# Operand parts side by side for each k-tile, and 18 more projection slabs in a two-matmul form

## The chip, the cores and the metric

The kernel runs on one core of a Trainium2 chip, in one launch. The metric is the device time of that launch in microseconds (us), as a median over runs. A core has five engines with a queue each: PE (TensorE, matmuls, with its weight loads shown apart as PEld), DVE (VectorE), ACT (ScalarE), POOL (GpSimd) and SP (which here issues transfers). Each engine works through its own queue in order and waits on semaphores for the others. SBUF is the on-chip memory with 128 partitions; PSUM holds what PE writes, in eight banks of 512 float32 a partition.

## What is computed

Two transformer blocks on 256 tokens of width 1024, all in float32. Rotary embedding, norms and the scan of the first layer are left out here.

```python
def reference(x, ...):
    x = first_block(x, ...)          # even layer (window attention + scan), FFN, odd layer, FFN
    return second_block(x, mem, ...)

def second_block(x, mem, ...):
    x = x + 0.5 * swiglu(rmsnorm(x, ffn1_norm), ffn1_w_gate, ffn1_w_up, ffn1_w_down)
    z = rmsnorm(x, mix_norm) @ w_in
    z_sgu = gelu(z[..., :2 * D_SGU])                 # gates u and values v
    ...                                              # q, k, v of the dilated attention
    y_a = chunked_spatial_gating(z_sgu, ...)
    y_b = dilated_mixture_attention(q, k, v)
    x = x + concatenate([rmsnorm(y_a), rmsnorm(y_b)]) @ w_out
    x = x + memory_cross_attention(rmsnorm(x), rmsnorm(mem), wq, wk, wv, wo)
    x = x + 0.5 * swiglu(rmsnorm(x, ffn2_norm), ffn2_w_gate, ffn2_w_up, ffn2_w_down)
    return rmsnorm(x, final_norm)

def memory_cross_attention(h, m, wq, wk, wv, wo):
    q, k, v = h @ wq, m @ wk, m @ wv                 # 4 heads of 256
    p = softmax(q @ k.T / 16)
    return (p @ v) @ wo
```

The odd layer of the first block is a stick-breaking attention: `A[t,s] = beta_ts * prod(1 - beta_tj)` over `s < j < t`, with the product done as a sum of softplus values that a matmul with a triangular matrix adds up. Four FFNs (gate, up, down; 2816 wide) hold most of the arithmetic.

## The kernel before

**Two parts for each number.** PE takes its operands in a rounded 32-bit type, so each float32 operand is held as a high and a low part, and a product is hi·hi + hi·lo + lo·hi. Weights come in slabs of 128 x 2048 (`slab`, transfer at L277); ACT casts each half of a slab to its high part `whi` (L293) and DVE subtracts to get `wlo` (L295), two slabs ahead of their use, in 5 buffers each. Both engines do this for every slab beside their other work. Activations are transposed: features on partitions, the 256 tokens along the free axis. An operand tile `a` is `[128, 2 parts, 4 k-tiles, 256]` (`operand`), two of them for the 1024 features; the hidden tiles `h0` to `h10` of an FFN are `[128, 2 parts, 2 k-tiles, 256]`.

**Two ways of a product.** `mm3` (L320 to L322) is three matmuls of 256 moving columns with a weight load each: whi·hi, whi·lo, wlo·hi. `mm2` (L366, L367) is two: wlo·hi with 256 columns, then whi against hi and lo at once with 512 columns, into a whole PSUM bank, whose second half then holds whi·lo and has to be added to the first. With the parts outermost in the tile, the 512 columns of L367 are two runs of 256. Only the FFNs use `mm2`; all other projections go through `gemm_feat` or `gemm_tok` with `mm3`. In `gemm_feat` one slab of 256 features fills one bank (the two blocks b of 128 features in its halves), half of the k-tiles first for both blocks, then the other half. One DVE multiplication by the norm's factors (`scaled`, L482; L1350 for the gates of the mix) takes it out of PSUM. In the FFN each block of 128 features has a bank of its own; `half` takes it out with an ACT copy of the second half (L525, into a tile `half` with 4 buffers) and a DVE addition (L526). In `gemm_tok` tokens are the stationary side and 512 weights lie contiguous as moving columns.

**Stages.** Even layer, FFN, odd layer, FFN, FFN, mix (spatial gating and dilated attention, with the memory's norm and the first of its projections between), cross attention, FFN, final norm. Strings give the order in which pieces are written: `ODD = "q0 k0 k1 q1 a00 k2 k3 l00 a01 l01 q2 q3 a10 ..."` (q, k, v: projections by slab; a: scores and softplus, L1191 to L1211; l: the triangular sums, L1218), `MIX = "x N v w y r0 r1 u0 10 u1 00 K0 11 g0 01 12 g1 13 K1 K2 K3"` (u: gates; two digits: steps of the dilated attention, L587 to L625; g: gating, L1357; N, K: the memory's norm and the cross attention's keys), `CROSS = "q0 q1 s00 s10 t00 t10 q2 v00 v10 q3 s11 s01 w0 ..."` (q: projections; s: scores L1408 and softmax L1413 to L1420; t: transposes of the probabilities, helper L401, with the copy out of PSUM at L1429; v: products with the values, L1440; w: output projection). A scheduler then sets every engine's final order from its own estimates, so the order in the program can differ from the strings.

**Banks.** `ps(tag)` hands out banks in turn: 2 with the tag `mm`, 4 `acc`, 2 `tr`. Projections, scores of the dilated attention and its q·k share `mm`; a new user waits until the user two before has been read out.

Of the kernel before, what the change touches and what calls it, by code (L numbers as in the profile page):

```python
# [8 lines left out]
F32 = mybir.dt.float32  # L9
F32R = mybir.dt.float32r  # L10
# [3 lines left out]
ALU = mybir.AluOpType  # L14
AX = mybir.AxisListType

P = 128
# [211 lines left out]
class Parts(tuple):  # L229


    def __new__(cls, x):
        self = super().__new__(cls, (x[:, 0], x[:, 1]))
        self.both = x
        return self


class Kernel:
# [85 lines left out]
    def operand(self, pool=None, tag="a"):  # L324

        if pool is not None:
            x = self.t(pool, [P, 2, 4, 256], tag, F32R)
        else:
            x = self.t(self.ap4, [P, 2, 4, 256], "a", F32R, bufs=self.A_BUFS)
        return Parts(x)  # L330

    def lhs(self, ops, k, t):
# [29 lines left out]
    def mm2(self, out, w, x, first, last):  # L362


        mm = self.nc.tensor.matmul
        mm(out[:, 0, :], w[1], x[:, 0], start=first, stop=False, skip_group_check=True)  # L366
        mm(out, w[0], x, start=False, stop=last, skip_group_check=True)  # L367

    def gemm_out(self, acc, w, ops, ks, first, last, done=None):

# [106 lines left out]
        rb, rs = self.inv_rms(sqs, D, 1e-6, tag)  # L477
        return ops, rb, rs

    def scaled(self, dst, rb):  # L480

        return lambda c, ps: self.nc.vector.tensor_tensor(  # L482
            dst[:, 2 * c:2 * c + 2, :], ps, rb.unsqueeze(1).to_broadcast([P, 2, 256]), ALU.mult)


    def memory(self, f, how, pool=None):
        nc = self.nc
        c = int(f[1:] or 0)
        if f[0] == "N":
            mem = self.t(self.wp, [P, 2048], "raw", bufs=2).rearrange("p (b t) -> p b t", b=8)  # L490
            self.load_feat(mem, self.a["mem"], nc.sync)
            self.mops, self.mrb, self.mrs = self.norm(mem, 8, "mrb", haste=False, pool=pool, soon=how[1])
        elif f[0] == "K":
            if not self.kt:
                self.kt = self.t(self.late, [P, 8, 256], "kt")
            self.gemm_feat(self.mops, "cross_wk", 0, c * 256, 256,
                           self.scaled(self.kt[:, 2 * c:2 * c + 2, :], self.mrb), how[0])
# [13 lines left out]


    def ffn(self, kind, layer, gain, factor):
        nc = self.nc
# [3 lines left out]
        rb2 = rb.unsqueeze(1).to_broadcast([P, 2, 256])  # L518
        hs = []

        def half(ps, dst):

            v = ps.rearrange("p (i t) -> p i t", i=2)
            y = self.t(fp, [P, 256], "half", bufs=4)
            nc.scalar.copy(y, v[:, 1])  # L525
            nc.vector.tensor_tensor(dst, v[:, 0], y, ALU.add)  # L526

        def products(name, c, tag, evac):
            w = self.slab(f"{kind}_{name}", layer, "f", 0, c * 256)
            for b in range(2):  # L530
                ps = self.ps(tag)
                out = ps.rearrange("p (i t) -> p i t", i=2)
                for k in range(8):
                    self.mm2(out, w(k * 256 + b * P, P), ops[k // 4].both[:, :, k % 4, :], k == 0, k == 7)
                evac(b, ps)

        for c in range(11):
            sg = self.t(fp, [P, 2, 256], "sg", bufs=2)
            h = self.t(fp, [P, 2, 256], "h", bufs=2)
            x = self.t(fp, [P, 2, 2, 256], f"h{c}", F32R)  # L540
            hs.append(x)

            products("gate", c, "acc", lambda b, ps, sg=sg: half(ps, sg[:, b]))
# [3 lines left out]
            products("up", c, "mm", lambda b, ps, h=h: half(ps, h[:, b]))  # L547
            nc.vector.tensor_tensor(h, h, sg, ALU.mult)
            nc.scalar.copy(x[:, 0], h)
            nc.vector.tensor_tensor(x[:, 1], h, x[:, 0].bitcast(F32), ALU.subtract)  # L550


        n = 0
        for o in range(8):
            ps = self.ps("acc")
            out = ps.rearrange("p (i t) -> p i t", i=2)
            for k in range(22):
                if n % 16 == 0:
                    w = self.slab(f"{kind}_down", layer, "d", n, 0, ahead=LASTF if n == 160 else None)
                self.mm2(out, w(n % 16 * P, P), hs[k // 2][:, :, k % 2, :], k == 0, k == 21)  # L560
                n += 1
            with self.tc.high_priority(offset=self.HASTE):
                y = self.t(fp, [P, 256], "y", bufs=2)
                x = self.xt[:, o, :]
                nc.vector.scalar_tensor_tensor(y, out[:, 0], factor, x, ALU.mult, ALU.add)
                nc.vector.scalar_tensor_tensor(x, out[:, 1], factor, y, ALU.mult, ALU.add)
        stack.close()


# [533 lines left out]
    def ssm_gate(self, ep, gy):  # L1103
        nc = self.nc
        flat = lambda x: x.rearrange("p a n -> p (a n)")
        yt = self.t(ep, [P, 8, 4, 32], "s1")
        hi, lo = self.operand()
        for h in range(2):
            ps = self.ps("tr")
            for t in range(4):  # L1110
# [46 lines left out]
    def odd(self):  # L1157
# [84 lines left out]
        for f in ODD.split():  # L1242
# [2 lines left out]
                toks(ops, "odd_w_in", 2048, c, v, rs)  # L1245
            elif f[0] in "kq":
                dst, base, r = (kt, 1024, rb) if f[0] == "k" else (qt, 0, rb8)
                self.gemm_feat(ops, "odd_w_in", 0, base + c * 256, 256,
                               self.scaled(dst[:, 2 * c:2 * c + 2, :], r), "acc" if f in OACC else "mm")
            elif f[0] == "a":  # L1250
                scores(*divmod(c, 10))
            elif f[0] == "l":
# [11 lines left out]
    def mix(self):  # L1264
# [80 lines left out]

        su = self.t(mp, [P, 4, 256], "su")

        def gates(c, ps):
            d = su[:, 2 * c:2 * c + 2, :]
            nc.vector.tensor_tensor(d, ps, rb.unsqueeze(1).to_broadcast([P, 2, 256]), ALU.mult)  # L1350
            nc.scalar.activation(d, d, AF.Gelu)

        def gating(t):
# [17 lines left out]
        for f in MIX.split():  # L1371
# [8 lines left out]
            elif f[0] == "r":  # L1380
                att[c] = dilated(c)
            elif f[0] == "u":
                self.gemm_feat(ops, "w_in", 0, c * 256, 256, lambda _, ps: gates(c, ps))
            elif f[0] == "g":
                gating(c)
            elif f[0] in "NKW":
# [7 lines left out]
    def cross(self):  # L1394
# [51 lines left out]
        for n, f in enumerate(CROSS.split()):  # L1446
            c = int(f[1])
            if f[0] == "q":
                self.gemm_feat(ops, "cross_wq", 0, c * 256, 256,
                               self.scaled(qt[:, 2 * c:2 * c + 2, :], rb), "mm" if c < CQ else "acc")  # L1450
            elif f[0] == "s":
                scores(c, int(f[2]))
            elif f[0] == "t":
# [105 lines left out]
```

## Time and profile before

| | |
|---|---|
| runs | 1245.78, 1247.03, 1249.15 us (median 1247.03) |
| profiled execution | 1243.83 us, its span on the core 1242.1 us |
| PE | busy 1211.7 us, 98% of the span, 7686 matmul records |
| DVE, ACT, POOL | 868.8 us (70%), 676.6 us (54%), 211.2 us (17%) |
| granted TensorE clock | 0.986 of full speed over the span; lower only in the first tenth |
| weights moved | 205.57 MB read from HBM, 167 GB/s |

The page divides the span in 40 slices of 31 us. From the fourth on PE shows the highest digit in every slice but the last, while DVE is at 5 to 8 tenths and ACT at 4 to 6. Matmuls are pipelined: the time that a row gives for one (0.28 us for 256 columns) is longer than the distance between the starts of two in a row, and that distance is what a stream costs. So matmuls are read below by start times. The chain that ended last lies on PE for 92% of the span.

### The profile page before, as it was taken

Reading aid. Unit: us, or ns where it says so; the run is one execution under the profiler, and the core shown is the slowest. Engines: PE = TensorE matmul, PEld = TensorE weight load, DVE = VectorE, ACT = ScalarE, POOL = GpSimd, SP = SyncE. Lnnn points to the kernel's source line nnn. Section 1 sums busy time; section 2 is a strip of 40 time slices with the busy share of each in tenths; the row PEclk is TensorE's granted clock in tenths of the full one; section 3 lists DMA queues with packets and bytes.
Section 4 is the critical chain, followed back from the end, with each engine's and each line's share of the span. In section 5 each row is a group of like instructions: output and inputs, shape, how many; then the busy total and the mean of one; then the engine's idle time right before and its main releaser. Section 6 shows DMA issues by size and latency. Waiting matters only on the chain.

```text
span 1242.1 us, 19044 instructions
## 1 busy us (share of the span) xinstructions
PE 1211.7 (98%) x7686; PEld 1072.7 (86%) x7686; DVE 868.8 (70%) x1191; ACT 676.6 (54%) x1052; POOL 211.2 (17%) x177
## 2 busy tenths in 40 slices
PE   6889999999999999999999999999999999999997
PEld 6777998888899879888888888888889999888886
DVE  8978588777665647877766867766866656777752
ACT  6543566565446755655545655545664545655542
POOL 7665021110010002101001110002201101111000
PEclk9978999999999999999999999999999999999998
DMA  6541355555553325455654545646633434555551
GB/s 208 172 158 53 139 172 194 180 201 203 180 197 110 131 68 204 170 187 186 216 191 174 196 177 198 204 174 212 209 131 103 155 118 139 190 183 201 204 200 38
DMA packets 36776, 208.86 MB, mean 168 GB/s; under 512 B 3920, under 2 KB 9808, under 8 KB 12752
## 3 DMA queue, kind: packets, MB, share of 16 engines
q1 hardware_dynamic: 35824, 205.48, 47.7%
q0 software_dynamic: 576, 1.64, 0.5%
q8 instruction: 60, 0.98, 0.3%
q10 hardware_dynamic: 288, 0.52, 0.1%
q14 instruction: 28, 0.23, 0.1%
HBM read 205.57 MB, written 2.06 MB: 167 GB/s over the span
## 4 chain that ended last, share of the span: by engine, by line
PE 92%; DVE 5%; DMA 1%; issue 1%; ACT 1%; POOL 0%; DVEq 0%; ACTq 0%
PE acc L367 26%; PE acc L366 13%; PE mm L367 13%; PE mm L366 7%; PE mm L320 4%; PE mm L322 4%; PE mm L321 4%; PE acc L322 4%; PE acc L321 4%; PE acc L320 4%; PE mm L591 1%; PE tr L401 1%; PE acc L1191 1%; DVE wlo L295 1%; PE acc L625 1%; DVE a L454 1%
## 5 line engine op out<-in xcount | busy, mean ns | idle before, releaser
L295 DVE TENSOR_TENSOR wlo<-raw,whi 128x1024 fp32r<-128x1024 f32 (+1 forms) x378 | 472.0, 1251 | 225.1 <-ACT whi L293 223.6
L293 ACT CAST whi<-raw 128x1024 fp32r<-128x1024 f32 (+1 forms) x378 | 392.4, 1043 | 280.8 <-DMA raw<-in_wts 111.2
L367 PE MATMUL acc<-h,whi 128*128 128x512 f32 x704 | 247.8, 397 | 0.0
L367 PE MATMUL mm<-a,whi 128*128 128x512 f32 x704 | 247.0, 392 | 0.0
L367 PE MATMUL acc<-a,whi 128*128 128x512 f32 x704 | 246.0, 392 | 0.0
L366 PE MATMUL acc<-h,wlo 128*128 128x256 f32 x704 | 196.9, 281 | 0.0
L366 PE MATMUL mm<-a,wlo 128*128 128x256 f32 x704 | 196.6, 281 | 0.0
L366 PE MATMUL acc<-a,wlo 128*128 128x256 f32 x704 | 196.3, 280 | 0.0
L367 PEld LDWEIGHTS acc<-h,whi 128*128 128x128 f32 x704 | 131.9, 188 | 32.0
L367 PEld LDWEIGHTS mm<-a,whi 128*128 128x128 f32 x704 | 131.5, 187 | 28.5
L367 PEld LDWEIGHTS acc<-a,whi 128*128 128x128 f32 x704 | 130.9, 187 | 28.2
L366 PEld LDWEIGHTS acc<-a,wlo 128*128 128x128 f32 x704 | 133.0, 189 | 1.0
L366 PEld LDWEIGHTS acc<-h,wlo 128*128 128x128 f32 x704 | 132.9, 189 | 0.3
L366 PEld LDWEIGHTS mm<-a,wlo 128*128 128x128 f32 x704 | 132.6, 189 | 0.2
L546 POOL TENSOR_TENSOR sg<-sg,rb 128x512 f32<-128x512 f32 x44 | 58.2, 1326 | 388.8 <-ACT sg L545 379.2
L463 POOL TENSOR_TENSOR ssq<-ssq,sq 128x512 f32<-128x512 f32 x26 | 39.7, 1528 | 416.7 <-ACT sq L461 253.2
L320 PE MATMUL mm<-a,whi 128*128 128x256 f32 x224 | 66.4, 298 | 6.7 <-ACT whi L293 6.7
L321 PE MATMUL acc<-a,whi 128*128 128x256 f32 x240 | 67.4, 284 | 0.0
L322 PE MATMUL acc<-a,wlo 128*128 128x256 f32 x240 | 67.1, 285 | 0.0
L322 PE MATMUL mm<-a,wlo 128*128 128x256 f32 x224 | 66.1, 296 | 0.8 <-DVE wlo L295 0.7
L320 PE MATMUL acc<-a,whi 128*128 128x256 f32 x240 | 66.0, 286 | 0.0
L321 PE MATMUL mm<-a,whi 128*128 128x256 f32 x224 | 65.8, 295 | 0.0
(371 smaller groups left out, 1951.5 us busy)
## 6 DMA issues: line engine op xcount, KB each, us to landing
raw<-in_wts SPq DMA_DIRECT2D x187, 1024.0 KB, 4.9
raw<-in_mem SPq DMA_DIRECT2D x4, 512.0 KB, 5.6
eb<-lag SPq DMA_DIRECT2D x4, 512.0 KB, 4.8
x<-in_x SPq DMA_DIRECT2D x4, 256.0 KB, 5.3
raw<-in_wts SPq DMA_DIRECT2D x4, 256.0 KB, 5.6
sprm<-in_prm SPq DMA_DIRECT2D x1, 512.0 KB, 9.1
ud<-s SPq DMA_DIRECT2D x1, 512.0 KB, 2.6
uu<-ud SPq DMA_DIRECT2D x8, 64.0 KB, 5.3
```

Source lines behind the costliest of these rows:

```text
L293: nc.scalar.copy(hi[:, c:c + n], src)
L295: nc.vector.tensor_tensor(lo[:, c:c + n], src, hi[:, c:c + n].bitcast(F32), ALU.subtract)
L320: mm(out, a[0], b[0], start=start, stop=False, skip_group_check=True)
L321: mm(out, a[0], b[1], start=False, stop=False, skip_group_check=True)
L322: mm(out, a[1], b[0], start=False, stop=stop, skip_group_check=True)
L366: mm(out[:, 0, :], w[1], x[:, 0], start=first, stop=False, skip_group_check=True)
L367: mm(out, w[0], x, start=False, stop=last, skip_group_check=True)
L401: self.nc.tensor.transpose(out, in_, self.ident[:k, :k])
L454: lo = nc.vector.scalar_tensor_tensor(lo, x[:, b, :], g, hi.bitcast(F32), ALU.mult, ALU.subtract).ins
L463: nc.gpsimd.tensor_tensor(ssq, ssq, q, ALU.add)
L546: nc.gpsimd.tensor_tensor(sg, sg, rb2, ALU.mult)
L591: nc.tensor.matmul(scv[:, i, :], qt[r, qb, t * P:(t + 1) * P], kt[r, kblock(qb), 0:keys], start=False, stop=(i == per - 1))
```

## The change

The operand tiles are laid out with the two parts of a k-tile side by side: `[128, 4 k-tiles, 2 parts, 256]`, and the hidden tiles of the FFN `[128, 2 k-tiles, 2 parts, 256]`. The 512 columns of the second matmul of `mm2` are then one run (`both(k)`). The projections `cross_wk` (4 slabs), `odd_w_in` for q and k (8), the two slabs of the mix's gates in `w_in`, and `cross_wq` (4) go from `gemm_feat` with `mm3` to `gemm_scaled`, which uses `mm2` as the FFN does: 18 slabs, 16 products of k-tile and block each. A slab then takes two banks, one for each block, one after the other. It is taken out with `halves` for each block, whose temporary now comes from the tag `sq` (2 buffers of 512, shared with the squares of the norms), and one multiplication in SBUF for both blocks. The FFNs call the same helpers. One tile of the even layer (`ssm_gate`) keeps the old layout.

```diff
 class Parts(tuple):
-        self = super().__new__(cls, (x[:, 0], x[:, 1]))
-        self.both = x
+        self = super().__new__(cls, (x[:, :, 0], x[:, :, 1]))
+        self.tile = x
         return self
+    def both(self, k):
+        return self.tile[:, k].rearrange("p i t -> p (i t)")
...
-            x = self.t(self.ap4, [P, 2, 4, 256], "a", F32R, bufs=self.A_BUFS)
+            x = self.t(self.ap4, [P, 4, 2, 256], "a", F32R, bufs=self.A_BUFS)
...
-        mm(out[:, 0, :], w[1], x[:, 0], start=first, stop=False, skip_group_check=True)
+        mm(out[:, :256], w[1], x[:, :256], start=first, stop=False, skip_group_check=True)
         mm(out, w[0], x, start=False, stop=last, skip_group_check=True)
+    def halves(self, ps, dst):
+        y = self.t(self.wk, [P, 512], "sq", bufs=2)[:, :256]
+        self.nc.scalar.copy(y, ps[:, 256:])
+        self.nc.vector.tensor_tensor(dst, ps[:, :256], y, ALU.add)
+    def gemm_wide(self, ops, name, layer, n0, dst, tag="mm"):
+        w = self.slab(name, layer, "f", 0, n0)
+        for b in range(2):
+            ps = self.ps(tag)
+            for k in range(8):
+                self.mm2(ps, w(k * 256 + b * P, P), ops[k // 4].both(k % 4), k == 0, k == 7)
+            self.halves(ps, dst[:, b])
...
-    def scaled(self, dst, rb):
-        return lambda c, ps: self.nc.vector.tensor_tensor(
-            dst[:, 2 * c:2 * c + 2, :], ps, rb.unsqueeze(1).to_broadcast([P, 2, 256]), ALU.mult)
+    def gemm_scaled(self, ops, name, layer, n0, dst, rb, tag="mm"):
+        self.gemm_wide(ops, name, layer, n0, dst, tag)
+        self.nc.vector.tensor_tensor(dst, dst, rb.unsqueeze(1).to_broadcast([P, 2, 256]), ALU.mult)
...
-            x = self.t(fp, [P, 2, 2, 256], f"h{c}", F32R)
+            x = Parts(self.t(fp, [P, 2, 2, 256], f"h{c}", F32R))
...
-        def gates(c, ps):
+        def gates(c):
             d = su[:, 2 * c:2 * c + 2, :]
-            nc.vector.tensor_tensor(d, ps, rb.unsqueeze(1).to_broadcast([P, 2, 256]), ALU.mult)
+            self.gemm_scaled(ops, "w_in", 0, c * 256, d, rb)
             nc.scalar.activation(d, d, AF.Gelu)
...
-                self.gemm_feat(ops, "cross_wq", 0, c * 256, 256,
-                               self.scaled(qt[:, 2 * c:2 * c + 2, :], rb), "mm" if c < CQ else "acc")
+                self.gemm_scaled(ops, "cross_wq", 0, c * 256, qt[:, 2 * c:2 * c + 2, :], rb,
+                                 "mm" if c < CQ else "acc")
```

With fewer matmuls to place, the scheduler sets other orders. In the FFNs PE's order is the same as before. PE's queue has 6897 rows before and 6608 after.

PE of the kernel before, in the cross attention, around the first scores (`mm` <- `kt`, `qt`, tiles 1661 and 1665; `acc_1686` is q's fourth slab; L401 transposes the probabilities that come of the scores):

```order
L322 MATMUL acc_1678_9756<-a_1637_9539,wlo_1653_9591 128x256
L1408 MATMUL mm_1661_9704<-kt_1543_8849,qt_1646_9581 128x256 x2
L1408 MATMUL mm_1665_9718<-kt_1543_8849,qt_1646_9581 128x256 x4
L320 MATMUL acc_1686_9838<-a_1636_9538,whi_1656_9646 128x256
L321 MATMUL acc_1686_9838<-a_1636_9538,whi_1656_9646 128x256
...
L322 MATMUL acc_1686_9838<-a_1637_9539,wlo_1659_9651 128x256
L401 MATMUL tr_1669_9732<-ident_6_80,prob_1664_9713 128x128 x4
```

The same place on PE after (L1409 are the scores, L419 the transposes, `acc_1739` the second block of q's fourth slab):

```order
L369 MATMUL acc_1739_9705<-a_1679_9413,wlo_1704_9516 128x256
L370 MATMUL acc_1739_9705<-a_1679_9413,whi_1703_9515 128x512
L1409 MATMUL mm_1713_9574<-kt_1573_8759,qt_1688_9455 128x256 x2
L1409 MATMUL mm_1709_9560<-kt_1573_8759,qt_1688_9455 128x256 x2
L419 MATMUL tr_1717_9588<-ident_6_80,prob_1712_9569 128x128 x4
L419 MATMUL tr_1721_9595<-ident_6_80,prob_1716_9583 128x128 x4
L1441 MATMUL mm_1730_9653<-probt_1718_9593,mv0_111_578 128x128
```

Before, 39 matmuls of q's fourth slab stand between the last scores and the first transposes; after, that slab stands ahead of the scores and nothing stands between.

DVE after, from the last addition of q's fourth slab to the first probabilities (L1414 to L1421 are the softmax, L298 is the low part of a weight slab, L501 q's multiplication):

```order
L376 TENSOR_TENSOR qt_1688_9455<-acc_1739_9705,sq_1740_9722 128x256
L1414 TENSOR_REDUCE mx2_1710_9565<-mm_1709_9560 128x2
L298 TENSOR_TENSOR wlo_1755_9761<-raw_1753_9758,whi_1754_9760 128x1024
L501 TENSOR_TENSOR qt_1688_9455<-qt_1688_9455,rb_1687_9453 128x512
L1415 TENSOR_SCALAR mx2_1710_9565<-mx2_1710_9565 128x2
L1414 TENSOR_REDUCE mx2_1714_9579<-mm_1713_9574 128x2
L1415 TENSOR_SCALAR mx2_1714_9579<-mx2_1714_9579 128x2
L1420 RECIPROCAL den2_1711_9566<-den2_1711_9566 128x2
L1421 TENSOR_TENSOR prob_1712_9569<-prob_1712_9569,den2_1711_9566 128x512
```

Before, DVE had no split and no multiplication between the first reduction and the first probabilities; after, one of each stands there.

PE after, in the mix, at the gates' second slab (`mm_1556` is the bank of the dilated attention's first scores; `mm_1565` and `mm_1567` are the two blocks of the slab, with `mm` handing out two banks in turn):

```order
L591 MATMUL mm_1556_8657<-kt_1456_8189,qt_1455_8188 128x256 x2
L369 MATMUL mm_1565_8690<-a_1440_8138,wlo_1524_8520 128x256
L370 MATMUL mm_1565_8690<-a_1440_8138,whi_1523_8519 128x512
...
L369 MATMUL mm_1567_8710<-a_1440_8138,wlo_1524_8520 128x256
L370 MATMUL mm_1567_8710<-a_1440_8138,whi_1523_8519 128x512
...
L419 MATMUL tr_1558_8669<-ident_6_80,prob_1557_8664 128x128 x4
L587 MATMUL mm_1569_8732<-dilh_1434_8124,identr_7_82 128x512
```

Before, the slab's 48 matmuls went into one bank and stood between the scores and the next user of the scores' bank (L587); after, the slab's second block is that next user, with 16 matmuls between.

## Rows read from the trace of the kernel before

**Rows 1.** The page: PE's share of the span, and the granted clock in 40 slices.

```profile
PE 1211.7 (98%) x7686; PEld 1072.7 (86%) x7686; DVE 868.8 (70%) x1191; ACT 676.6 (54%) x1052; POOL 211.2 (17%) x177
...
PEclk9978999999999999999999999999999999999998
```

**Rows 2.** Timeline of PE: start, us, engine, line, tiles, columns; two-matmul pairs with operand `a`.

```profile
230.11 0.28 PE L366 MATMUL mm<-a,wlo 128*128 128x256 f32 x1
230.23 0.39 PE L367 MATMUL mm<-a,whi 128*128 128x512 f32 x1
...
236.01 0.28 PE L366 MATMUL acc<-a,wlo 128*128 128x256 f32 x1
```

**Rows 3.** Timeline of PE in the down projection of the first FFN.

```profile
289.05 0.28 PE L366 MATMUL acc<-h,wlo 128*128 128x256 f32 x1
...
296.67 0.40 PE L366 MATMUL acc<-h,wlo 128*128 128x256 f32 x2
...
345.04 0.28 PE L366 MATMUL acc<-h,wlo 128*128 128x256 f32 x1
...
350.34 0.28 PE L366 MATMUL acc<-h,wlo 128*128 128x256 f32 x1
```

**Rows 4.** Timeline of PE, three-matmul products in the odd layer's first projection.

```profile
351.05 0.28 PE L320 MATMUL mm<-a,whi 128*128 128x256 f32 x1
...
351.77 0.28 PE L320 MATMUL mm<-a,whi 128*128 128x256 f32 x1
```

**Rows 5.** Timeline of PE, matmuls with 512 contiguous moving columns.

```profile
419.27 0.39 PE L321 MATMUL mm<-wlo,a 128*128 128x512 f32 x1
...
424.94 0.39 PE L322 MATMUL mm<-whi,a 128*128 128x512 f32 x1
```

**Rows 6.** Groups from 350 us to 1045 us: busy, mean ns | idle before; bank read-outs.

```profile
L526 DVE TENSOR_TENSOR h<-mm,half 128x256 f32<-128x256 f32 x44 | 18.1, 414 | 0.0
...
L525 ACT COPY half<-mm 128x256 f32<-128x256 f32 x44 | 16.1, 365 | 7.9 <-PE mm L367 7.7
...
L482 DVE TENSOR_TENSOR qt<-mm,rb 128x512 f32<-128x512 f32 x6 | 4.0, 683 | 0.7 <-PE mm L322 0.7
```

**Rows 7.** Waits of PE from 350.6 to 1045.4 us: total, times, longest.

```profile
PE acc L625 <- ACT prob L619: 1.1, 2, 0.7
```

**Rows 8.** Timeline of the cross attention's first scores and softmax.

```profile
1002.69 1.46 PE L1408 MATMUL mm<-kt,qt 128*128 128x256 f32 x6
...
1003.97 0.68 DVE L1413 TENSOR_REDUCE mx<-mm 128x2 f32<-128x512 f32 x1
...
1006.19 0.69 DVE L1420 TENSOR_TENSOR prob<-prob,den 128x512 f32<-128x512 f32 x1
...
1007.10 0.69 DVE L1420 TENSOR_TENSOR prob<-prob,den 128x512 f32<-128x512 f32 x1
...
1008.65 0.60 PE L401 MATMUL tr<-ident,prob 128*128 128x128 f32 x4
```

**Rows 9.** Timeline of the mix at the dilated attention's first scores.

```profile
903.78 1.13 PE L591 MATMUL mm<-kt,qt 64*128 64x256 f32 x4
...
905.32 1.23 DVE L295 TENSOR_TENSOR wlo<-raw,whi 128x1024 fp32r<-128x1024 f32 x1 [0.82 <-ACT whi L293]
...
909.55 0.20 ACT L605 ACTIVATION_READ_ACCUMULATOR prob<-mm,mneg 128x1 f32 x1
...
910.68 0.40 PE L587 MATMUL mm<-dilh,identr 128*128 128x512 f32 x1
```

**Rows 10.** Timeline of the mix: the sum of a norm's squares.

```profile
928.13 0.73 POOL L1310 TENSOR_TENSOR sq<-sq 128x256 f32<-128x256 f32 x1 [40.08 <-ACT sq L1309]
```

**Rows 11.** Timeline of the odd layer's first scores, softplus and triangular sums.

```profile
378.69 1.60 PE L1191 MATMUL acc<-qt,kt 64*128 64x128 f32 x12
...
385.83 1.13 ACT L1210 CAST sph<-sp 128x512 fp32r<-128x512 f32 x2
...
390.40 0.40 PE L1218 MATMUL acc<-sph,trih 128*128 128x512 f32 x1
```

More of the change, by code (lines that the diff above doesn't have):

```diff
@@ L326, in operand @@
         if pool is not None:
-            x = self.t(pool, [P, 2, 4, 256], tag, F32R)
+            x = self.t(pool, [P, 4, 2, 256], tag, F32R)
         else:
-            x = self.t(self.ap4, [P, 2, 4, 256], "a", F32R, bufs=self.A_BUFS)
+            x = self.t(self.ap4, [P, 4, 2, 256], "a", F32R, bufs=self.A_BUFS)
         return Parts(x)
@@ L495, in memory @@
                 self.kt = self.t(self.late, [P, 8, 256], "kt")
-            self.gemm_feat(self.mops, "cross_wk", 0, c * 256, 256,
-                           self.scaled(self.kt[:, 2 * c:2 * c + 2, :], self.mrb), how[0])
+            self.gemm_scaled(self.mops, "cross_wk", 0, c * 256, self.kt[:, 2 * c:2 * c + 2, :], self.mrb, how[0])
         else:
@@ L519, in ffn @@
         hs = []
[L521 to L535, printed above, removed]
         for c in range(11):
@@ L539, in ffn @@
             h = self.t(fp, [P, 2, 256], "h", bufs=2)
-            x = self.t(fp, [P, 2, 2, 256], f"h{c}", F32R)
+            x = Parts(self.t(fp, [P, 2, 2, 256], f"h{c}", F32R))
             hs.append(x)
-            products("gate", c, "acc", lambda b, ps, sg=sg: half(ps, sg[:, b]))
+            self.gemm_wide(ops, f"{kind}_gate", layer, c * 256, sg, "acc")
             nc.vector.tensor_tensor(sg, sg, rb2, ALU.mult)
@@ L546, in ffn @@
             nc.gpsimd.tensor_tensor(sg, sg, rb2, ALU.mult)
-            products("up", c, "mm", lambda b, ps, h=h: half(ps, h[:, b]))
+            self.gemm_wide(ops, f"{kind}_up", layer, c * 256, h)
             nc.vector.tensor_tensor(h, h, sg, ALU.mult)
-            nc.scalar.copy(x[:, 0], h)
-            nc.vector.tensor_tensor(x[:, 1], h, x[:, 0].bitcast(F32), ALU.subtract)
+            nc.scalar.copy(x[0], h)
+            nc.vector.tensor_tensor(x[1], h, x[0].bitcast(F32), ALU.subtract)
         n = 0
@@ L555, in ffn @@
             ps = self.ps("acc")
-            out = ps.rearrange("p (i t) -> p i t", i=2)
             for k in range(22):
@@ L559, in ffn @@
                     w = self.slab(f"{kind}_down", layer, "d", n, 0, ahead=LASTF if n == 160 else None)
-                self.mm2(out, w(n % 16 * P, P), hs[k // 2][:, :, k % 2, :], k == 0, k == 21)
+                self.mm2(ps, w(n % 16 * P, P), hs[k // 2].both(k % 2), k == 0, k == 21)
                 n += 1
@@ L564, in ffn @@
                 x = self.xt[:, o, :]
-                nc.vector.scalar_tensor_tensor(y, out[:, 0], factor, x, ALU.mult, ALU.add)
-                nc.vector.scalar_tensor_tensor(x, out[:, 1], factor, y, ALU.mult, ALU.add)
+                nc.vector.scalar_tensor_tensor(y, ps[:, :256], factor, x, ALU.mult, ALU.add)
+                nc.vector.scalar_tensor_tensor(x, ps[:, 256:], factor, y, ALU.mult, ALU.add)
         stack.close()
@@ L1106, in ssm_gate @@
         yt = self.t(ep, [P, 8, 4, 32], "s1")
-        hi, lo = self.operand()
+        x = self.t(self.ap4, [P, 2, 4, 256], "a", F32R, bufs=self.A_BUFS)
+        hi, lo = x[:, 0], x[:, 1]
         for h in range(2):
@@ L1247, in odd @@
                 dst, base, r = (kt, 1024, rb) if f[0] == "k" else (qt, 0, rb8)
-                self.gemm_feat(ops, "odd_w_in", 0, base + c * 256, 256,
-                               self.scaled(dst[:, 2 * c:2 * c + 2, :], r), "acc" if f in OACC else "mm")
+                self.gemm_scaled(ops, "odd_w_in", 0, base + c * 256, dst[:, 2 * c:2 * c + 2, :], r,
+                                 "acc" if f in OACC else "mm")
             elif f[0] == "a":
@@ L1382, in mix @@
             elif f[0] == "u":
-                self.gemm_feat(ops, "w_in", 0, c * 256, 256, lambda _, ps: gates(c, ps))
+                gates(c)
             elif f[0] == "g":
```

## The prediction

> **What bounds the kernel now.** I read the page first: PE is busy 98% of the span, at full granted clock in all slices but the first few [rows 1]. So a price is paid on PE, either as the distance between the starts of two matmuls or as a gap in its queue. The next view is therefore PE's timeline, read by start times. A pair of `mm2` on operand `a` runs in 5.90 us / 17 = 347 ns over 17 pairs [rows 2]. In the down projection 22 pairs run in 7.62 us, 346 ns each; at 296.67 two matmuls of 256 follow each other, since there PE's order breaks the alternation, and from then to the end of the stage the pairs run slower, 15 of them in 5.30 us, 353 ns each [rows 3]. So the two-run operand is not slow as such; it falls into a slower rhythm after a broken alternation and stays there. A triple of `mm3` takes 0.72 us / 2 = 360 ns, so 120 ns for 256 columns [rows 4], and a contiguous 512 takes 5.67 us / 25 = 227 ns [rows 5]. At last I read PE's waits between the second FFN's neighbours: in the odd layer, the mix and the cross attention they come to little over a microsecond [rows 7]. These stages are covered almost without a gap, and how much cover each wait has is the question for this change.
>
> **The matmuls removed.** 18 slabs of 16 products go from 360 to 347 ns: 288 x 13 ns = **-3.7 us**. No column is saved; 512 + 256 stream as before, and what goes is the start of one matmul (two of 120 against one of 227). The Trainium skill ("TensorE: Matmul & The Clock Gate", section "Back-to-back issue gap") gives a lone matmul N/2.4 + 2.5 ns, by which the removal would be worth 288 x 2.5 ns, an estimate of 0.7 us; rows 4 and 5 show a larger fixed part, 13 ns over N/2.4, and I go by them.
>
> **The layout.** Contiguous parts give 120 + 227 = 347 ns, what the two-run pair already takes in its fast rhythm. What they may end is the slow one. Its price is 353 - 347 = 6 ns on 704 - 4 x 22 = 616 pairs of the four down projections (8 x 22 x 4), taking the other three like the one shown: **3.7 us**. For its end speaks that streams with one shape of contiguous rows hold 227 ns [rows 5]; against it, that I see no contiguous 512 alternate with 256. I give the end a little better than even. FFN orders don't change, so nothing else moves there.
>
> **Read-outs.** A slab's one DVE multiplication (0.68 us) becomes two ACT copies (0.37), two DVE additions (0.41) and the multiplication [rows 6]: 0.73 us of ACT and 0.83 of DVE in each 5.6 us slab. Both engines have room on the average [rows 1], so the sum of it costs nothing. Where a chain through them releases PE it counts, and so do the shorter distances in PE's new order. Those are the next three terms.
>
> **Cross attention.** Before, the first reduction starts at 1003.97 and the first probabilities end at 1006.88, 2.91 us later; the second end at 1007.79; the transposes stand at 1008.65, behind q's fourth slab [rows 8]. After, that slab is ahead of the scores, and PE has nothing between. DVE has in the same chain a split (1.23 us) [rows 9] and q's multiplication (0.69) [rows 6]: 2.91 + 1.23 + 0.69 = 4.8 us from the reduction, which can start about when PE issues its last score. PE stands about 4.8 us; the second transposes come 0.9 us after the first, whose own 0.36 us fill a part, so 0.5 more. **+5.4 us**. Bounds: 3 (split and multiplication turn out to lie elsewhere) and 6.
>
> **Mix.** Before, the first scores' bank is released by the last exponential at 909.75, and PE comes back to it at 910.68, after 48 matmuls in the 5.8 us since the scores [rows 9]. After, the second block of the gates' slab needs that bank when 16 matmuls, 2.8 us, have passed: 904.9 + 2.8 = 907.7, against 909.75. That is 2.0 us, and 2.4 with the other block's copy and addition ahead in the queues. The same for the first key slab behind the next exponentials, with a shorter chain, 0.7. Later in the stage transposes, the product with the values and the norm's sums stand in direct sequence; each pair waits for an ACT copy as L625 does already, 0.7 at worst [rows 7], two of them 1.4; a third waits for a square on ACT and an addition on POOL, some 0.7 each [rows 7, 10], 1.4. The place of the 1.1 us before falls away, of which I take back 0.7. **+5.2 us**, bounds 2 and 8 (from one such wait to all with the splits in the chain).
>
> **Odd layer.** Scores end at 380.3 and the first `sph` at 386.4: 6.1 us, covered four times over since the sums come at 390.40 [rows 11]. After, 15 pairs (5.2 us) and a few scores are left between, so 0.7 us, and up to 1.8 with the new addition and copy ahead. **+1.2 us**, bounds 0 and 3.5.
>
> **The sum.** New waits 5.4 + 5.2 + 1.2 = 11.8; with -3.7 that is **+8.1 us** where the slow rhythm stays and **+4.4 us** where it ends. On the profiled execution's 1243.83 that gives 1248.2; against the median of the runs, which lies 3.2 us above that execution, 1247.03 + 4.4 = **1251.4 us**.
>
> **Rivals.**
> - *The slow rhythm stays.* Then 1247.03 + 8.1 = 1255.1. For it: the break in the FFN's order is still there. Against: rows 5.
> - *Contiguous columns are faster than the fast rhythm; the kernel gets faster.* In a two-run pair the 256 takes 0.12 and the 512 the rest, 347 - 117 = 230 ns [rows 2]; if the 230 holds 3 ns for the second run and contiguous rows give 117 + 227 = 343, all 2112 pairs of the FFNs and the 288 new ones gain 3.8 ns, 9.1 us: 1251.4 - 9.1 = 1242.3. From 3.4 ns a pair on it is faster by more than 0.3% (4.4 + 3.7 = 8.1 us over 2400 pairs). For it: 230 against 227. Against: 256 in a stream takes 120, not 117 [rows 4], so the 3 ns seem only to change sides. The Trainium skill ("Advanced Engine Details and Errata", section "PSUM Cachelines") says that non-contiguous access patterns slow matmuls markedly, which would put the result here; the fast two-run pairs of rows 2 don't bear it out for this operand, the slow ones of rows 3 may.
> - *The cover is there after all.* The waits are half of what I sum, 5.9, because ACT and DVE run further ahead: 1247.03 + 8.1 - 5.9 - 3.7 = 1245.5 with the slow rhythm gone; no change. For it: both engines are at two thirds. Against: in the cross attention PE's order leaves nothing to run.
> - *All pairs fall into the slow rhythm*, if a contiguous 512 meets a 256 badly: 6 ns on 1408 + 288 more pairs and no gain, 1255.1 + 10.2 = 1265.3.
>
> That the change doesn't do what it says is no rival: PE's queue loses 289 rows.
>
> **How the numbers follow.** Likeliest is the forecast, new waits with the slow rhythm gone, 40%; the rhythm stays, 30%; contiguous faster, 12%; cover, 14%; all slow, 4%. A measurement of this kernel can tell about 0.3%, 3.7 us, from no change. The forecast lies just beyond that, and its waits are uncertain by some 4 us: 0.24 slower, 0.15 same, 0.01 faster. The second gives 0.27 and 0.03; the third 0.09 faster, 0.03 same; the fourth 0.10 same, 0.04 faster; the last 0.04 slower. Together 0.14 faster, 0.31 same, 0.55 slower. The range goes from 1243.0 (the third at its weaker end) to 1258.0 (the second with its waits 3 us longer).
>
> **What would show it.** The pairs in the down projection after the broken alternation: 347 or 353 ns. The waits of PE: a gap of 4 to 5 us ahead of L419 at the first transposes of the cross attention, some 2 us ahead of L369 in the mix with the scores' exponentials as releaser, below 2 us ahead of L1219 in the odd layer. The products of k in q and k slabs: 347 ns. It would be wrong if the cross gap is under 3 us, if pairs anywhere run under 344 ns, or if DVE or ACT turn up as releasers inside the FFNs, where I count none.

## The result and the profile after

The changed kernel is slower: 1260.59 us median (1259.22 to 1263.7, four runs) against 1246.4 (1243.48 to 1249.15, four runs), a ratio of 1.0118 with a 95% interval of 1.0087 to 1.0148. The forecast was 1251.4 with a range up to 1258.0: the direction was right, the size was not, +14.2 us where +4.4 was forecast.

The head of the page after, to lay beside [rows 1]:

```profile
PE 1215.9 (96%) x7398; PEld 1061.3 (84%) x7398; DVE 877.2 (70%) x1227; ACT 689.0 (55%) x1088; POOL 210.3 (17%) x177
...
PE   5889999999999999999999999999988989999997
PEld 5777998888888789888888888888777979888886
```

288 matmuls are gone, and yet PE is busy as long as before; its share of the span falls. The late eights in the row of slices stand at the mix and the cross attention. To see where the time went I cut both traces at the down projections, which lie on PE in all kernels here (line L366 before and L369 after, operand `h`). All cuts are starts of matmuls, in us:

| stretch | before | after | |
|---|---|---|---|
| start to first down projection (even layer, gate and up) | 288.7 | 293.6 | +4.9 |
| the first down projection | 61.8 | 61.8 | 0 |
| its end to the second down projection (odd layer, gate and up) | 251.4 | 251.5 | +0.1 |
| end of the third to the fourth (mix, cross attention, gate and up) | 318.6 | 333.5 | +14.9 |

The first line is no effect of the change: no instruction of the even layer changes place, and the same stretch took 293.6 us in the profile of one kernel below that runs faster than before, 288.6 in another. The rest of the difference, and with it the median's 14.2 us, lies in the last line. At the first product of the cross attention's q it splits into the mix, 132.4 us before and 140.2 after (+7.8), and the cross attention, 63.2 and 70.3 (+7.1); gate and up take 123.0 in both. The mix can't be read more closely than 2 us: with the order of before it took 132.4 to 134.4 us in five profiles, the most with the new layout alone. The cross attention took 63.2 us in all that have its q in three matmuls. PE's waits in the mix and the cross attention, from 855 to 1066 us (what PE waited for, us in total, times, longest); before, there were the 1.1 us of [rows 7] and the last row below, with the same length:

```profile
PE tr L419 <- DVE prob L1421: 4.2, 2, 3.9
PE mm L369 <- ACT prob L605: 3.5, 2, 2.5
PE acc L625 <- ACT prob L619: 2.6, 4, 1.0
PE tr L437 <- POOL sq L1311: 1.6, 1, 1.6
PE mm L370 <- DVE a L472: 1.2, 1, 1.2
PE mm L369 <- ACT vt L1378: 0.6, 1, 0.6
PE mm L587 <- ACT prob L605: 0.3, 1, 0.3
```

The first row is the cross attention's gap. Its timeline, to lay beside [rows 8] (start, us, engine, line, operation, tiles; the idle time before it and its releaser in brackets):

```profile
1022.22 1.24 PE L1409 MATMUL mm<-kt,qt 128*128 128x256 f32 x5
...
1022.63 0.69 DVE L1414 TENSOR_REDUCE mx<-mm 128x2 f32<-128x512 f32 x1 [0.25 <-PE mm L1409]
1023.31 1.23 DVE L298 TENSOR_TENSOR wlo<-raw,whi 128x1024 fp32r<-128x1024 f32 x1
1024.45 0.68 DVE L501 TENSOR_TENSOR qt<-qt,rb 128x512 f32<-128x512 f32 x1
...
1026.55 0.69 DVE L1421 TENSOR_TENSOR prob<-prob,den 128x512 f32<-128x512 f32 x1
...
1027.39 0.65 PE L419 MATMUL tr<-ident,prob 128*128 128x128 f32 x4 [3.93 <-DVE prob L1421]
...
1028.30 1.09 PE L419 MATMUL tr<-ident,prob 128*128 128x128 f32 x4 [0.26 <-DVE prob L1421]
...
1033.76 1.89 PE L1409 MATMUL mm<-kt,qt 128*128 128x256 f32 x8
```

The split and the multiplication stand inside the softmax's chain, as the order had it: 1022.63 to 1027.24 is 4.6 us, 2.91 before. What I had not counted comes behind it. PE's granted clock in that place (two microseconds a row; busy time and count of PE, PEld, DVE, ACT and POOL, then the clock, the DMA share and GB/s):

```profile
1024.00:1026.00 2.00, 0.00 (x0) 0.00 (x0) 1.97 (x5) 0.70 (x3) 0.00 (x0) 1.00 0.96 406
1026.00:1028.00 2.00, 0.61 (x4) 0.42 (x4) 1.57 (x5) 1.23 (x6) 0.00 (x0) 0.97 0.09 37
1028.00:1030.00 2.00, 1.74 (x9) 1.73 (x9) 0.15 (x1) 1.16 (x2) 0.00 (x0) 0.50 0.00 0
1030.00:1032.00 2.00, 2.00 (x15) 2.00 (x14) 0.00 (x0) 0.01 (x1) 0.00 (x0) 0.68 0.00 0
```

After the gap the granted clock is 0.50, the lower of its two levels (1.2 of 2.4 GHz), until 1031.3, and the second transposes and the first products run at half speed. The same happens in the mix, behind the wait for the square's sum at 957.99 (timeline of PE):

```profile
957.99 0.61 PE L437 MATMUL tr<-ones,sq 128*128 128x1 f32 x4 [1.55 <-POOL sq L1311]
958.46 0.36 PE L369 MATMUL mm<-m,wlo 128*128 128x256 f32 x1
...
960.21 0.41 PE L369 MATMUL mm<-m,wlo 128*128 128x256 f32 x1
960.42 0.63 PE L370 MATMUL mm<-m,whi 128*128 128x512 f32 x1
960.85 0.41 PE L369 MATMUL mm<-m,wlo 128*128 128x256 f32 x1
...
962.77 0.63 PE L323 MATMUL acc<-a,whi 128*128 128x256 f32 x3
```

A pair takes 0.64 us there (960.21 to 960.85) instead of 0.35; the eight pairs of the block take 962.77 - 958.46 = 4.3 us instead of 2.8. In the kernel before the clock is not lowered anywhere between the even layer and the last FFN's end; it is lowered behind that, from 1234.9 us on, so not only in the first tenth.

### The profile page after: what moved, and what is told of

Read it like the earlier page. It is cut to its first block, busy times and chain, and to the rows that moved or that the text cites. A ratio compares the mean times of both kernels' runs of the same rounds, so it can differ in the third digit from the quotient of the medians.

```text
span 1262.0 us, 18523 instructions
## 1 busy us (share of the span) xinstructions
PE 1215.9 (96%) x7398; PEld 1061.3 (84%) x7398; DVE 877.2 (70%) x1227; ACT 689.0 (55%) x1088; POOL 210.3 (17%) x177
## 4 chain that ended last, share of the span: by engine, by line
PE 82%; DVE 6%; ACT 5%; DMA 4%; issue 2%; POOL 0%; SPq 0%; DVEq 0%; ACTq 0%
PE acc L370 24%; PE mm L370 14%; PE acc L369 13%; PE mm L369 8%; DMA raw<-in_wts 4%; PE acc L323 3%; PE acc L324 3%; PE acc L325 3%; DVE wlo L298 2%; ACT whi L296 2%; PE mm L323 2%; PE mm L325 2%; PE mm L324 2%; PE tr L419 1%; PE mm L591 1%
## 5 line engine op out<-in xcount | busy, mean ns | idle before, releaser
L298 DVE TENSOR_TENSOR wlo<-raw,whi 128x1024 fp32r<-128x1024 f32 (+1 forms) x378 | 469.6, 1245 | 245.2 <-ACT whi L296 243.2
L370 PE MATMUL mm<-a,whi 128*128 128x512 f32 x880 | 309.7, 393 | 1.2 <-DVE a L472 1.2
L370 PE MATMUL acc<-a,whi 128*128 128x512 f32 x752 | 263.1, 392 | 0.0
L369 PE MATMUL mm<-a,wlo 128*128 128x256 f32 x880 | 246.3, 282 | 3.1 <-ACT prob L605 2.5
L369 PE MATMUL acc<-a,wlo 128*128 128x256 f32 x752 | 210.3, 281 | 0.0
L369 PE MATMUL acc<-h,wlo 128*128 128x256 f32 x704 | 196.9, 281 | 0.6 <-ACT h L550 0.6
L370 PEld LDWEIGHTS mm<-a,whi 128*128 128x128 f32 x880 | 164.3, 187 | 37.3 <-DVE a L472 1.6
L369 PEld LDWEIGHTS mm<-a,wlo 128*128 128x128 f32 x880 | 165.7, 189 | 5.3 <-ACT prob L605 2.8
L370 PEld LDWEIGHTS acc<-a,whi 128*128 128x128 f32 x752 | 140.0, 187 | 30.1
L369 PEld LDWEIGHTS acc<-a,wlo 128*128 128x128 f32 x752 | 142.0, 189 | 0.8
L369 PEld LDWEIGHTS acc<-h,wlo 128*128 128x128 f32 x704 | 132.9, 189 | 1.2 <-ACT h L550 0.9
L375 ACT COPY sq<-mm 128x256 f32<-128x256 f32 x118 | 43.1, 367 | 34.6 <-PE mm L370 29.3
L550 ACT CAST h<-h 128x512 fp32r<-128x512 f32 x44 | 27.4, 622 | 58.4 <-DVE h L549 57.9
L546 ACT ACTIVATE sg<-sg 128x512 f32<-128x512 f32 x44 | 27.7, 632 | 50.2 <-DVE sg L545 48.1
L324 PE MATMUL acc<-a,whi 128*128 128x256 f32 x192 | 53.4, 284 | 0.0
L323 PE MATMUL acc<-a,whi 128*128 128x256 f32 x192 | 51.1, 285 | 0.0
```

What stands on the lines that cost most here:

```text
L298: nc.vector.tensor_tensor(lo[:, c:c + n], src, hi[:, c:c + n].bitcast(F32), ALU.subtract)
L323: mm(out, a[0], b[0], start=start, stop=False, skip_group_check=True)
L324: mm(out, a[0], b[1], start=False, stop=False, skip_group_check=True)
L369: mm(out[:, :256], w[1], x[:, :256], start=first, stop=False, skip_group_check=True)
L375: self.nc.scalar.copy(y, ps[:, 256:])
L550: nc.scalar.copy(x[0], h)
```

## The experiments

The times are medians over runs, but for `fill`, which ran once; the kernel before ran beside them on the same chip, with a median of 1246.2 to 1247.0. Theory W in the expectations is what the last section reads out of the trace: waits of PE that lost their cover, and the clock behind them.

**The layout alone.** The 18 slabs are in three matmuls again; the FFNs keep the new layout and the new helpers.

```diff
+            self.gemm_feat(self.mops, "cross_wk", 0, c * 256, 256,
+                           self.scaled(self.kt[:, 2 * c:2 * c + 2, :], self.mrb), how[0])
...
+                self.gemm_feat(ops, "cross_wq", 0, c * 256, 256,
+                               self.scaled(qt[:, 2 * c:2 * c + 2, :], rb), "mm" if c < CQ else "acc")
```

(the same for the odd layer's q and k and for the gates)

> The new operand layout alone; the 18 slabs go back to three matmuls of 256 columns and one multiplication, PE's order is that of the kernel before. Theory W (the loss of 14 us lies in waits of PE that lost their cover in the mix and the cross attention, and in the clock after them): no change, 1246.4 within 3 us, each down projection 61.7 us from its first to its last matmul as before. Theory L (the layout itself costs, as the even stage suggests, which was 4.9 us longer in the profile of after with the same order on PE): 1251. The forecast's own hope, that contiguous rows end the slow rhythm: 1242.7, down projections 60.8 us.

1246.84 us (ten runs), ratio 1.0000 (0.9986 to 1.0014): no effect of the layout shows. The down projection, to lay beside [rows 3]:

```profile
344.91 0.28 PE L369 MATMUL acc<-h,wlo 128*128 128x256 f32 x1
...
350.21 0.28 PE L369 MATMUL acc<-h,wlo 128*128 128x256 f32 x1
```

5.30 us for 15 pairs, 353 ns, the same as with two runs: contiguous rows don't end the slow rhythm. The even layer's stretch is 288.6 us here, so the 4.9 us of the table are not the layout's. In the mix PE waits 0.8 us ahead of L323 for ACT's `vt` here, so the 0.6 us of that kind in the changed kernel need not be the two matmuls' doing.

**The old layout with the new form.**

```diff
-        self = super().__new__(cls, (x[:, :, 0], x[:, :, 1]))
+        self = super().__new__(cls, (x[:, 0], x[:, 1]))
...
-        return self.tile[:, k].rearrange("p i t -> p (i t)")
+        return self.tile[:, :, k]
```

> The 18 slabs in two matmuls as in the change, but the parts outermost in the tiles as before, so the 512 moving columns are two runs of 256; orders are those of the changed kernel. Theory W: as the changed kernel, 1260.6 within 4 us, pairs at 347 ns where nothing broke the alternation. Theory L: 1256. If contiguous columns are what makes a pair cheap, the new pairs take more than 347 ns and the time is above 1262.

1260.38 us, ratio 1.0121 (1.0098 to 1.0143), as the whole change. So all of the loss comes from the new form of the projections and the orders that go with it. The pairs with two runs, in the gates' second block:

```profile
912.17 0.28 PE L369 MATMUL mm<-a,wlo 128*128 128x256 f32 x1
...
913.90 0.28 PE L369 MATMUL mm<-a,wlo 128*128 128x256 f32 x1
```

1.73 us for five pairs, 346 ns.

**Only the odd layer's slabs in two matmuls.** The diff is that of the first experiment without its part for q and k of the odd layer.

> New layout, and of the 18 slabs only the 8 of the odd layer's q and k in two matmuls; mix and cross attention have the orders of before. Theory W: 1246.4 - 1.7 (8 x 16 x 13 ns) + 1.3 (0.5 ahead of the triangular sums, 0.8 ahead of the output projection) = 1246, no change. Theory L: 1251.

1248.7 us, ratio 1.0024 (1.0009 to 1.0039), 1.9 us above the kernel before and just measurable; 1246 was expected. The stretch from the first to the second down projection took 253.3 us, not 251.4. The odd layer has no more waits than expected; the gate and up pairs of the FFN behind it run in the slow rhythm for a part of it: 304 of the 1461 pairs with operand `a` that could be read in this profile are over 349 ns, 57 of 1350 were before. Other kernels with the same order there (the changed one among them) took 251.3 to 251.9 us in seven profiles and 253.5 and 253.6 in two. What sets off the slow rhythm there is open.

The second down projection of this profile shows that a broken alternation does not always start the slow rhythm. It takes 61.0 us, not 61.8: its pairs come in slow and are fast behind the break:

```profile
603.51 0.28 PE L369 MATMUL acc<-h,wlo 128*128 128x256 f32 x1
...
607.05 0.28 PE L369 MATMUL acc<-h,wlo 128*128 128x256 f32 x1
...
662.28 0.28 PE L369 MATMUL acc<-h,wlo 128*128 128x256 f32 x1
...
664.36 0.28 PE L369 MATMUL acc<-h,wlo 128*128 128x256 f32 x1
```

Ten pairs in 3.54 us, 354 ns, then six in 2.08, 347. The profiles of `no_mix` and `fill` show the same.

**Each part of the rest taken back.** In `no_crossq` q of the cross attention goes back to three matmuls, in `no_mix` the gates and the memory's keys, in `keys_only` the gates, in `gates_only` the keys; the diffs are the parts of the first one.

> The changed kernel, but the cross attention's q (4 slabs) in three matmuls again; PE's order there is that of before, q's fourth slab between the first scores and the first transposes. Theory W: the cross attention's 7.1 us are gone, 1260.6 - 7.1 = 1253.5, and PE waits under 0.5 us ahead of the first transposes. Rival M (the loss is in the mix alone, and what the cross attention shows is what was displaced): 1260.

1253.73 us, ratio 1.0065 (1.0034 to 1.0097). PE's waits from 850 us on:

```profile
PE mm L369 <- ACT prob L610: 3.5, 2, 2.5
PE acc L630 <- ACT prob L624: 2.6, 4, 1.0
PE tr L437 <- POOL sq L1316: 1.5, 1, 1.5
...
```

The wait for the cross attention's probabilities is gone, those of the mix stand, and the time is that of theory W; its rival's 1260 is excluded.

> The changed kernel, but the gates and the memory's keys (6 slabs, all that stands in the mix) in three matmuls again. Theory W: the mix's 7.8 us are gone, 1252.8, the wait of 4.2 us in the cross attention stays. Rival C (all of it is the cross attention): 1260.

1254.08 us, ratio 1.0066 (1.0038 to 1.0093), with eight runs from 1249.6 to 1259.6:

```profile
PE tr L419 <- DVE prob L1427: 4.2, 2, 3.9
...
PE acc L631 <- ACT prob L625: 1.1, 2, 0.7
```

The mirror image: the cross attention's wait stands; of the mix's there are left those of [rows 7] and a few more that are small, the largest 1.0 us for `vt` (0.8 in `layout_only`).

> The changed kernel, but the gates' 2 slabs in three matmuls again, so that in the mix only the memory's 4 key slabs are in two. Theory W: the wait of 2.5 us for the scores' bank goes with the gates, the ones further on (1.0, 1.0 and 1.6 us) stay or move with the order: 1260.6 - 3.0 = 1257.6. Rival: the gates cost nothing of their own, and the wait comes back at the first key slab: 1260.

1257.55 us, ratio 1.0105 (1.0066 to 1.0145).

> The changed kernel, but the memory's 4 key slabs in three matmuls again, so that in the mix only the gates are in two. Theory W: the wait of 2.5 us for the scores' bank stays, the waits after the last key slabs and the half clock behind them go: 1260.6 - 4.8 = 1255.8. Rival: all follows from the gates' wait, 1260.

1256.12 us, ratio 1.0069 (1.0042 to 1.0095). Both came within half a microsecond of theory W, but their runs spread by more, so that the two don't tell which of the mix's parts costs more; the interval of `keys_only`, 1254.5 to 1264.3 us, doesn't exclude its rival's 1260 either, that of `gates_only` does. Their traces do tell which wait goes with which: without the gates PE has no wait ahead of L369 for the scores' exponentials, without the keys no wait ahead of L437. Their mixes take 138.1 and 136.6 us, between the 140.2 of the changed kernel and the 132.4 to 134.4 of the old order.

**The cross attention's cover given back.** All 18 slabs stay in two matmuls; q's fourth slab is held back until the first scores are issued (`last[1, 0]` is the last matmul of the scores of the first two heads).

```diff
+                with self.tc.issue_after(after) if after is not None else nullcontext():
+                    self.mm2(ps, w(k * 256 + b * P, P), ops[k // 4].both(k % 4), k == 0, k == 7)
...
-                                 "mm" if c < CQ else "acc")
+                                 "mm" if c < CQ else "acc", last[1, 0] if c == 3 else None)
```

> The changed kernel with all 18 slabs in two matmuls, and one edit: q's fourth slab is held back until the first scores are issued, so that its 32 matmuls of 5.5 us stand between the scores and their transposes. Theory W: it is the order and not the form that costs there; the wait of 4.2 + 0.5 us falls to under 0.5, the clock stays up, 1260.6 - 4.7 - 1.7 = 1254. Rival R (the form costs: copies and additions for q in the queues of ACT and DVE delay the softmax by as much as is covered): the wait stays over 3 us, 1259.

1255.34 us, ratio 1.0086 (1.0056 to 1.0117). PE's timeline from the scores (L1411) to the products with the values (L1443):

```profile
1010.56 2.93 PE L1411 MATMUL mm<-kt,qt 128*128 128x256 f32 x12 [0.52 <-DVE qt L376]
...
1018.88 1.03 PE L420 MATMUL tr<-ident,prob 128*128 128x128 f32 x8
1020.99 1.27 PE L1443 MATMUL mm<-probt,mv 128*128 128x128 f32 x9 [1.08 <-ACT probt L1432]
```

No wait is left ahead of the transposes, and the clock stays up in this stage. Two smaller ones are new, 0.5 us ahead of the scores and 1.1 us between the transposes and the products, where before other matmuls stood between; 1.2 us for a normed operand (L473), earlier in q, are left as in the changed kernel. So more than half of the stage's loss was the order's: by the medians 5.3 us came back with the form unchanged, by the profiles the stage takes 66.5 us instead of 70.3. It still takes 3.3 us more than the 63.2 with three matmuls: in this kernel the form, with the waits that are left, does not pay there. By the medians `no_crossq` is 1.6 us faster, which these runs can't tell from zero.

**The gap filled with matmuls that nothing reads.** Twelve of 512 columns stand between the scores and the transposes; the transposes overwrite what they write.

```diff
+            for k in range(12 if (t, hp) == (0, 0) else 0):
+                with self.tc.issue_after(last[1, 0]):
+                    nc.tensor.matmul(tp, self.lhs(ops, k % 8, 0)[0], ops[k % 8 // 4].both(k % 4), start=True, stop=True)
```

> The changed kernel, with 12 matmuls of 512 columns that nothing reads put on PE between the first scores and their transposes in the cross attention, 2.7 us of work inside the wait of 4.2 us; the transposes overwrite what they write. Theory K (PE's idle time there is what lowers its granted clock behind it): no half clock after that wait, the transposes start as late as in the changed kernel, the stretch from the first transposes to the last of the first 32 products with the values takes 4.6 us instead of 6.3, 1.7 us. Rival (the clock falls there whatever PE does in the wait): 6.3 us.

1262.7 us in its one run, made for the trace. The clock at the place of the gap:

```profile
1024.00:1026.00 2.00, 2.00 (x10) 1.65 (x9) 2.00 (x4) 0.27 (x1) 0.00 (x0) 1.00 0.90 356
1026.00:1028.00 2.00, 0.88 (x6) 0.44 (x5) 1.53 (x6) 1.66 (x8) 0.00 (x0) 1.00 0.28 119
1028.00:1030.00 2.00, 1.72 (x15) 1.51 (x14) 0.58 (x1) 1.17 (x2) 0.00 (x0) 1.00 0.00 0
1030.00:1032.00 2.00, 2.00 (x20) 2.00 (x19) 0.17 (x1) 0.58 (x1) 0.00 (x0) 1.00 0.00 0
```

Full clock throughout. From the first transposes to the scores behind the products:

```profile
1027.82 0.63 PE L419 MATMUL tr<-ident,prob 128*128 128x128 f32 x4 [1.12 <-DVE prob L1422]
...
1032.80 1.89 PE L1410 MATMUL mm<-kt,qt 128*128 128x256 f32 x8
```

That is 5.0 us, where the changed kernel takes 1033.76 - 1027.39 = 6.4: 1.4 us of half clock, a little less than expected: with work in the gap the clock stays up, so it is PE's idle time that lowers it. The other profiles agree. In the five with this wait uncovered (the changed kernel, `old_layout`, `no_mix`, `keys_only`, `gates_only`) the clock fell in it or within 1.5 us behind it; in `no_crossq` and `cross_cover`, which have other matmuls there, it did not. The kernel as a whole was no faster: in this run the clock fell behind the mix's first wait too (0.50 from 916 to 918 us), where it had stayed up in the changed kernel's profile, and the FFN behind the odd layer had the slow rhythm.

**The broken alternation in the down projection.** In the kernel before, only the order of writing changed, so that the first bank's products of the last hidden tile come ten pairs later:

```diff
+        todo = [(o, k) for o in range(8) for k in range(22)]
+        todo[20:32] = todo[22:32] + todo[20:22]
...
+        for o, k in todo:
```

> The kernel before, with one edit in the FFNs: the products of the last hidden tile in the first bank of the down projection are written ten pairs later, when both its parts are there, so that PE's order keeps alternating 256 and 512 columns. Theory B (the broken alternation starts the slow rhythm): all down pairs at 347 ns, each stage 61.0 us instead of 61.8 or less, 3 to 3.7 us faster in all, 1243. Rival (the slow rhythm belongs to the stage, its additions to x, its slabs): down pairs at 353 ns from about the same time on, 1246.4.

1243.0 us, ratio 0.9967 (0.9949 to 0.9985). The first down projection, to lay beside [rows 3]:

```profile
300.17 0.28 PE L366 MATMUL acc<-h,wlo 128*128 128x256 f32 x1
...
354.25 0.28 PE L366 MATMUL acc<-h,wlo 128*128 128x256 f32 x1
```

54.08 us for 156 pairs, 346.7 ns, to the stage's end; the stage takes 60.8 us instead of 61.8 (354.36 against 293.58, 350.46 against 288.70). None of the 699 pairs of this kind that could be read is over 349 ns, 381 of 691 were before. Four stages give 3.8 us by the medians. It is faster than both the kernel before and the changed one.

**Both together:** the odd layer in two matmuls, the layout, and the mended order.

> New layout, the odd layer's 8 slabs in two matmuls, and the down projection's order mended. If the two add up: 1243.0 + 1.9 = 1244.9 by the runs of each alone. If the odd layer's extra 2 us were a matter of the slow rhythm, it is mended too: 1241.5.

1241.75 us, ratio 0.9972 (0.9948 to 0.9996). It is faster than before too, and not to be told from the mended order alone. Its stretch between the first two down projections is 251.3 us, in the fast rhythm.

## Why the prediction was right or wrong

- **The matmuls removed (-3.7 us).** Right in kind, too large: pairs take 347 ns in the converted slabs in the fast rhythm, with either layout, so a start costs 13 ns. But the slow rhythm is in these slabs too: 99 of their 224 pairs that could be read in the profile after, leaving out waits and half clock, are over 349 ns, and the mean is 350.7. That makes 288 x 9.3 ns, 2.7 us. By the rule in the Trainium skill ("TensorE: Matmul & The Clock Gate", section "Back-to-back issue gap") it would have been 2.5 ns a matmul; the rows decide, with 13.
- **The layout (-3.7 us).** Wrong, and this is the step that failed first. I took an end of the slow rhythm by contiguous rows for a little better than even, from rows with one shape of matmul; the experiment shows no difference at all (1.0000) and 353 ns as before. The slow rhythm starts at the broken alternation that [rows 3] show, and mending that ends it (`ffn_fix`). The forecast's likeliest case should have been the rival in which the rhythm stays, 1255.1.
- **The faster rival** falls with the same run: with or without two runs a pair takes the same. The rule on non-contiguous access patterns in the Trainium skill ("Advanced Engine Details and Errata", section "PSUM Cachelines") stands in a section on PSUM, and I had laid it on an operand in SBUF. For that operand, two runs of 1 KB, the layout's ratio of 1.0000 shows no such cost; the PSUM side was one run in both layouts, so no run here shows the rule at work.
- **Cross attention (+5.4).** The wait is 3.93 + 0.26 us by the list, 4.7 us by start times, so the term was good. The stage lost 7.1 us: another wait of 1.2 us for a normed operand (L472) earlier in q, which I had not seen, and 1.4 us of half clock. With the 0.8 us that q's slabs save these make 6.5; what the other 0.6 are is open.
- **Mix (+5.2).** Mis-sized: the waits there come to 10.4 us by start times against 2.1 before, so +8.3, just past my upper bound of 8. The wait for the scores' bank was 2.7 (2.4 forecast), for the first key slab 1.2 (0.7); but later in the stage there are four waits for L619's copies and one of 1.8 us for the sum of squares, of which I had counted three in all and taken too much of before's away. The largest, for the scores' bank, follows from PE's order as forecast: from the end of the scores to the last exponential it is 5.4 us (4.8 before), and the 16 matmuls between cover 2.8. But no run gives the mix its cover back in the new form, as `cross_cover` does, so that the order is to blame there is read from the trace alone. With 1.5 us of half clock and less 1.25 us for six slabs that makes 8.5; the stage's count is 7.8, and since that varies by 2 us with the order unchanged, and has the wait for `vt` with three matmuls too, the form's own part may be as little as 6.
- **Odd layer (+1.2).** Right in size, in part by luck: 0.5 us ahead of the triangular sums, for which 0.7 to 1.8 were forecast, and 0.8 ahead of the output projection, which I had not counted; with the saving it comes out at +0.1. The sums were not covered four times over before, as I wrote: 10.1 us stood over a chain of 6.1.
- **The clock.** Not in the sum at all, and the other step that failed: about 3 us, 1.5 in the mix and 1.4 in the cross attention. A wait in a stage that had been dense cost more than its length.
- **The sum.** 8.1 with the rhythm as before, 3.1 more in the mix, 2.9 for the clock, together 14.1; measured 14.2. So close a fit is luck: the smaller saving would add 1.0 and the wait for L472 1.2, and the mix is known to 2 us.
- **The rival that the cover is there after all** fell: the order showed nothing to run, and there was nothing.
- **A sign of being wrong came up.** I counted no wait for ACT or DVE inside the FFNs. The second down projection after has one, where the last hidden tile comes:

```profile
615.64 0.51 PE L369 MATMUL acc<-h,wlo 128*128 128x256 f32 x2 [0.59 <-ACT h L550]
```

It cost nothing, since the pairs behind it ran in the fast rhythm: the stage takes 61.7 us, 61.8 before. In `no_crossq` the same wait is followed by the slow rhythm, and the stage takes 62.5.

## What to carry to other kernels

Where PE is full, an order that covers waits is worth more than matmuls saved: 288 fewer matmuls gave back some 3 us and lost some 17 us of cover and clock. Look at what stands between a bank's last write and its next user before and after the edit, above all where a product now takes two banks of two. And look for places where two shapes of matmul stop alternating: four breaks of a few rows, one in each down projection, slowed some 600 pairs behind them by 6 ns each.

## What the runs showed of the hardware

- Pairs of 256 and 512 columns run in one of two rhythms, 347 and 353 ns, and can keep the slow one for tens of microseconds after the alternation was broken once; 54 us in the first down projection. In the third it ends before the stage does, at 842.8 us of 850, behind eight matmuls of one column. The same break, met in the slow rhythm, was followed by the fast one in three profiles (`odd_only`, `no_mix`, `fill`). Why is open. Contiguous or two-run operands make no difference to it. Streams of 256 columns alone take 120 ns, of 512 alone 227.
- PE's idle time of 4.2 us was followed by a stretch at a granted clock of 0.50 (1027.9 to 1031.3 us), and the wait of 1.6 us at 956 to 958, with others close ahead of it, by another (959.6 to 963.0). After the 2.5 us wait at 913 it stayed up in the changed kernel's profile and those of `old_layout` and `cross_cover`, and fell in those of three others with the same wait. Work that nothing reads, put into the gap, kept the clock up.
- The stretch up to the first down projection took 287.4 to 295.0 us in the profiles of kernels with the same instructions there; the granted clock in the even layer differs between them (0.71 and 0.50 from 93 to 108 us in the profiles before and after).
